# A hybrid convolution / mLSTM layer in float32: output projection by Strassen-Winograd pairs, branch stages reordered, small matmuls issued in groups

## The chip, the cores and the metric

The kernel runs on one core of a Trainium2 chip. Its time is the device time of one execution in microseconds (us); the time of before is the median of three runs, 2753.09 us (2752.79 to 2756.44). All durations below come from one profiled execution of the kernel before, which took 2749.06 us itself. Engines: PE is TensorE (matmuls), PEld its weight loads, DVE VectorE, ACT ScalarE, POOL GpSimd, SP the engine whose queue issues nearly all DMAs here.

## What is computed

One layer over 2048 tokens of 1024 channels. An input projection of some 11,000 columns feeds a gated short convolution (branch A) and a bidirectional chunked mLSTM with eight heads (branch B). Each branch has its own projection, gates merge them, and one output projection and a residual follow:

```python
y_a = b_a * conv * jax.nn.silu(z_a)
y_b = jax.nn.sigmoid(o) * hn * jax.nn.silu(z_b)
merged = jax.nn.sigmoid(g_a) * (y_a @ w_pa) + jax.nn.sigmoid(g_b) * (y_b @ w_pb)
out = merged @ w_out + b_out
x = x + gate[:, None, :] * out
return rmsnorm(x, g_final)
```

## The kernel before

Tokens are worked off in two halves of 1024. Every large product is done in float32 by splitting each operand into a rounded part and a rest (`split`, L178: an ACT cast, then a DVE or POOL subtract) and adding three matmuls, `PASSES`. One such matmul has a 128x128 weight and 512 moving columns; it is called a dense matmul below.

The input projection uses the seven products of Strassen-Winograd instead of eight (`pair`, L368; `Stream`, L293 makes the weight combinations on POOL, `total`, and splits them). A pair covers 256 output columns and one half of the tokens in 7x4x3 = 84 dense matmuls. Three PSUM banks X, Y, Z of the pool `pd` take the products in the order XYXYZYZ. The token combinations (`Tokens`, 14 pairs of buffers among `x0` to `x27`) are made once per half. For half 1 they go through DRAM (`prep_b`, `xod`).

The two branch projections (`branch`, `slab`, L419) and the output projection (`output`, L1292) do all eight block products. For each of eight column tiles (or token tiles) there are two accumulations of 8x3 = 24 dense matmuls, so 384 for each of the six stages at the end. Their moving operands are split once per stage into eight pairs of buffers (`Branch`, L1222), region 0 in `x0` to `x15`, region 1 in `x16` to `x27` and five to eight small buffers. The stages of before come in this order: branch A of half 1, branch B of half 1, output of half 1, branch A of half 0, branch B of half 0, output of half 0. `Branch(...)` issues all loads and splits of a stage in one block of code between two stages.

Beside the dense matmuls run the generators of two queues, `urgent` and `later`. `run(dense, rate, urate)` (L117) takes `rate` steps of `later` and `urate` steps of `urgent` per dense matmul; a step is the stretch of code up to the next `yield`. So the order on PE is fixed by these rates and yields. The order on the other engines is set by the scheduler, save for instructions that are held by `pin`. The longest generator is `scan` (L714), the emitting mLSTM pass: 64 chunks of 128 tokens (8 heads, 8 chunks) for each half. One chunk does a state update (L607, on a weighted copy `vw` that POOL makes at L602), scores (L764), four matmuls into `pn` (L813, L815), and, for four chunks at a time, four transposes (`finish`, L779). POOL masks the weights of two chunks (`mask`, L750) when their DMA `mw` has landed, and after that makes the next `vw`. These matmuls are in plain float32, have 128 or 129 columns and are called small below. In before, the scan of half 1 runs beside the input projection of half 1, and the scan of half 0 beside the first four of the six last stages.

## Time and profile before

| | |
|---|---|
| median of three runs | 2753.09 us |
| profiled execution, its own time | 2749.06 us |
| its span (first to last instruction) | 2747.3 us |
| PE busy | 2629.4 us, 96% |
| DVE, POOL, ACT busy | 61%, 42%, 39% |
| input projection of half 0, of half 1 | up to about 1070 us, up to about 2075 us |
| scan of half 0 | about 2075 to 2550 us |
| last stage | about 2655 to 2740 us |

A row of the windows view gives, for a stretch, its length, the busy time and (in brackets) the number of instructions on PE, PEld, DVE, ACT and POOL, the granted share of the TensorE clock, the DMA engines' share and their GB/s. A matmul's shown duration overlaps that of the next, so the price of one is read from the count in a full stretch or from the start times. A float32 small matmul shows as two records (x2), a transpose as one.

### The profile page before, as it was taken

To read this page: it belongs to the slowest core of one execution; us is meant where nothing else is said; L and a number is where in the kernel's file an instruction comes from. 1 tells how busy PE (TensorE), PEld (TensorE's weight loads), DVE (VectorE), ACT (ScalarE), POOL (GpSimd) and SP (SyncE) were. 2 spreads that over 40 slices of the span, in tenths; PEclk is the share of its full clock that TensorE was granted. 3 is DMA by queue.
4 is the path that set the end of the run, shared out by engine and by line. 5 is a ranking of instruction groups with operands and counts; after the bars stand their busy time and mean duration, and the time that the engine had idled before them with its cause. 6 is when DMAs were issued, how large, how long until landed. Compare 5 with 4: busy or idle time off the path is not lost. (4 is left out here: it accounts for less than half of the span.)

```text
span 2747.3 us, 38077 instructions
## 1 busy us (share of the span) xinstructions
PE 2629.4 (96%) x12715; PEld 2162.8 (79%) x12715; DVE 1673.9 (61%) x3022; ACT 1062.8 (39%) x2151; POOL 1160.4 (42%) x1387
## 2 busy tenths in 40 slices
PE   4799999999999999999999999999999998989998
PEld 3588888787788887787888888888888786778887
DVE  6743237688966657477677577568546554565423
ACT  6433334333344435343444444444445332332211
POOL 3521213363555542235555555545532354553123
PEclk8799999999999999999999999999999999999999
DMA  7223334363534557335545545644548777766753
GB/s 256 77 77 115 106 105 127 112 233 104 192 113 125 171 180 234 96 103 160 170 126 156 170 130 155 173 130 145 188 161 299 244 252 239 240 229 208 236 182 106
DMA packets 361659, 454.93 MB, mean 166 GB/s; under 512 B 24008, under 2 KB 261752, under 8 KB 361464
## 3 DMA queue, kind: packets, MB, share of 16 engines
q1 hardware_dynamic: 361072, 452.41, 51.9%
q8 instruction: 101, 1.65, 0.3%
q14 instruction: 94, 0.77, 0.1%
q10 hardware_dynamic: 392, 0.10, 0.0%
HBM read 324.08 MB, written 128.34 MB: 165 GB/s over the span
## 5 line engine op out<-in xcount | busy, mean ns | idle before, releaser
L384 PE MATMUL pd<-x,wh 128*128 128x512 f32 x4928 | 1628.4, 405 | 27.9 <-DVE u L393 12.5
L384 PEld LDWEIGHTS pd<-x,wh 128*128 128x128 f32 x4928 | 906.2, 189 | 215.2 <-DVE u L393 18.2
L384 PE MATMUL pd<-x,wl 128*128 128x512 f32 x2464 | 993.2, 403 | 0.8 <-DVE wl L180 0.8
L384 PEld LDWEIGHTS pd<-x,wl 128*128 128x128 f32 x2464 | 466.3, 189 | 87.9 <-DVE wl L180 1.2
L179 ACT CAST wh<-sw 128x512 fp32r<-128x512 f32 x352 | 218.1, 620 | 464.8 <-PE pd L384 402.9
L180 DVE TENSOR_TENSOR wl<-sw,wh 128x512 fp32r<-128x512 f32 x352 | 290.8, 827 | 173.0 <-ACT wh L179 172.5
L179 ACT CAST wh<-wr 128x512 fp32r<-128x512 f32 x328 | 203.2, 620 | 426.6 <-PE pd L384 290.8
L429 PE MATMUL pd<-x,wh 128*128 128x512 f32 x896 | 300.9, 420 | 2.1 <-DVE x L180 1.6
L328 POOL TENSOR_TENSOR sw<-wr,sw 128x512 f32<-128x512 f32 x88 | 120.5, 1369 | 430.8 <-DVE wl L180 427.1
L602 POOL TENSOR_SCALAR vw<-tk,wk 128x129 f32<-128x129 f32 x272 | 207.2, 770 | 189.9 <-DMA tk<-tokd 127.8
L180 DVE TENSOR_TENSOR wl<-wr,wh 128x512 fp32r<-128x512 f32 x328 | 258.7, 789 | 32.9 <-ACT wh L179 32.5
L328 POOL TENSOR_TENSOR sw<-wr 128x512 f32<-128x512 f32 x88 | 121.4, 1380 | 182.1 <-DVE wl L180 165.7
L429 PE MATMUL pd<-x,wl 128*128 128x512 f32 x448 | 172.3, 395 | 0.0
L429 PEld LDWEIGHTS pd<-x,wh 128*128 128x128 f32 x896 | 150.9, 191 | 21.2 <-DVE x L180 2.5
L846 DVE TENSOR_TENSOR t2k<-pd,u 128x512 f32<-128x512 f32 x168 | 115.5, 687 | 69.0 <-PE pd L384 67.3
L1312 PE MATMUL pd<-x,wh 128*128 128x512 f32 x448 | 152.1, 421 | 0.0
L250 POOL TENSOR_SCALAR ssq<-ssq 128x1 f32<-128x1 f32 x128 | 37.9, 296 | 240.9 <-ACT hf L829 236.0
L827 ACT ACTIVATE hf<-pn,rd 128x128 f32<-128x128 f32 x128 | 46.8, 366 | 239.4 <-DVE rd L823 161.9
L328 POOL TENSOR_TENSOR sw<-sw,wr 128x512 f32<-128x512 f32 x88 | 121.2, 1377 | 42.3 <-DVE wl L180 32.8
L328 POOL TENSOR_TENSOR sw<-wr,wr 128x512 f32<-128x512 f32 x88 | 127.4, 1448 | 15.4 <-DMA wr<-in_w_in_dram 10.0
L750 POOL TENSOR_SCALAR_AFFINE_SELECT mw<-mw 128x256 f32<-128x256 f32 x128 | 57.0, 465 | 177.4 <-DMA mw<-mwd 122.1
L813 PEld LDWEIGHTS pn<-tk,pt 128*128 128x128 f32 x512 | 95.8, 189 | 24.8 <-DVE pt L766 2.5
(276 smaller groups left out, 3716.8 us busy)
## 6 DMA issues: line engine op xcount, KB each, us to landing
wr<-in_w_in_dram SPq DMA_DIRECT2D x176, 512.0 KB, 3.9
mw<-mwd SPq DMA_DIRECT2D x64, 512.0 KB, 5.2
tk<-tokd SPq DMA_DIRECT2D x64, 386.0 KB, 4.1
tk<-tokd SPq DMA_DIRECT2D x64, 257.0 KB, 3.0
qkd<-t2k SPq DMA_DIRECT2D x64, 256.0 KB, 3.0
qk<-qkd SPq DMA_DIRECT2D x64, 256.0 KB, 3.4
tokd<-t2k SPq DMA_DIRECT2D x32, 258.0 KB, 3.3
tokd<-tk SPq DMA_DIRECT2D x64, 129.0 KB, 3.2
```

What stands on the lines that cost most here:

```text
L179: nc.scalar.copy(hi, raw)
L180: (eng or nc.vector).tensor_tensor(lo, raw, hi.bitcast(F32), op=OP.subtract)
L250: nc.gpsimd.tensor_scalar(dst, ss, 1.0 / n, EPS, op0=OP.mult, op1=OP.add)
L328: nc.gpsimd.tensor_tensor(s, a, b, op=op)
L384: nc.tensor.matmul(ps[b], op[wi][:, kk, :], xs.at(o, xi, kk), start=(fresh and kk + pi == 0), stop=(o == last[b] and kk == 3 and pi == 2), ...
L429: nc.tensor.matmul(pss[j], ops[k // 4][wi][:, k % 4, :], y(xi, k, j), start=(n + pi == 0), stop=(n == NK - 1 and pi == 2))
L602: pin(nc.gpsimd.tensor_scalar(vw, tk[:, VT], wk, None, op0=OP.mult))
L750: pin(nc.gpsimd.affine_select(mws[m][:, :, 0, d, :], mws[m][:, :, 0, d, :], pattern=[[0, 2], [s, P]], base=0, channel_multiplier=-s, compa ...
L813: nc.tensor.matmul(pn[:, d, :], pt[:, d, :], tk[:, VT], start=True, stop=False)
L827: nc.scalar.activation(hf, pn[:, 0, 0:P], AF.Copy, scale=rd[:, 0:1])
L846: nc.vector.tensor_tensor(t, ps, add, op=OP.add)
L1312: nc.tensor.matmul(pss[j], ops[k // 4][a][:, k % 4, :], wo(b, k, j), start=(k + pi == 0), stop=(k == NK - 1 and pi == 2))
```

## The change

- The output projection is done by `pair`: 8 pairs of token tiles, 7 products of 4x3 dense matmuls, 672 where 768 stood. Its fixed operand, `w_out` with the gate multiplied in, is stored by blocks (`wod`), three combinations are formed in DRAM by `combine` (the code that `prep_b` already had, now a function) beside the input projection of half 0, and it is loaded and split once, for both halves (`Operands`, the old `Tokens` with a loader).
- The order at the end is now A of half 1, B of half 1, A of half 0, B of half 0, then one output stage for both halves, half 1 first.
- `Branch` has a generator `fetch`: it issues the load of one block, waits 12 steps, then splits, with the casts held by `pin`. From the second branch stage on, operands come through `urgent` during the stage before. Gates and partial sums of a column tile are loaded when its accumulation begins (`PaEnd.begin`, `PbEnd.begin`), not when it ends.
- The scan of half 0 is split: heads 0 to 2 run beside the input projection of half 1, heads 3 to 7 beside the first three branch stages. The rates are 0.34 for 0.255 there, and 0.305 for 1/3 in the branch stages.
- Yields between single small matmuls are gone: four transposes come in a row, the four `pn` matmuls come in a row, and update and scores of the next chunk come in a row; `gap(4)` stands between such groups.

The core of the diff:

```diff
-    class Tokens:
+    class Operands:
...
+        def load(self, src, os):
+            for o in os:
+                for q in range(2):
+                    load_split(self.t[o][0][q], self.t[o][1][q], src[self.PLACE[o], :, 2 * q:2 * q + 2, :])
...
+    def combine(src, tile):
...
@@ scan
                 update(new, cur, tk, sp[n][2], g[carried]["dec"][:, j:j + 1])
-                yield
             if n + 1 < len(flat):
-                if n % 2:
-                    yield
                 start(n + 1)
-                yield
+            yield from gap(4)
             pt, qw, _ = sp.pop(n)
...
             for d in range(2):
                 nc.tensor.matmul(pn[:, d, :], pt[:, d, :], tk[:, VT], start=True, stop=False)
-                yield
                 nc.tensor.matmul(pn[:, d, :], qw[:, d, :], cur if d == carried else tk[:, ST], start=False, stop=True)
-                yield
+            yield from gap(4)
...
-        run(pair(st, xB, fin), 0.8 if w in ("q0", "o0", "z0") else 0.255, 0.5)
+        run(pair(st, xB, fin), 0.8 if w in ("q0", "o0", "z0") else 0.34, 0.5)
...
             later.extend([state_scan(sp_, hs, 1), scan(sp_, hs, 1)])
+            if r < EARLY:
+                later.append(scan(sp_, [r], 0))
...
-    def output(half, wo, misc):
...
+    later.append(scan(sp_, range(EARLY, NH), 0, lambda h: heads_done(h)))
+    RATE, URATE = 0.305, 0.3
...
+    ya = Branch(0, lambda k: yad[1][k])
+    yb = Branch(1, lambda k: ybd[1][k], ())
+    urgent.extend(yb.fetch(k) for k in range(NK))
+    run(branch(w_pa, ya, PaEnd, 1), RATE, URATE)
+    flush(urgent)
+    ya = Branch(0, lambda k: yad[0][k], ())
+    urgent.extend(ya.fetch(k) for k in range(NK))
+    run(branch(w_pb, yb, PbEnd, 1), RATE, URATE)
+    flush(urgent)
+    yb = Branch(1, lambda k: ybd[0][k], ())
+    urgent.extend(yb.fetch(k) for k in ready)
...
+    run(branch(w_pa, ya, PaEnd, 0), RATE, 0.5)
+    flush(later)
+    flush(urgent)
...
+    urgent.extend(load_wo(o) for o in range(4))
+    run(branch(w_pb, yb, PbEnd, 0), 0, 0.3)
+    flush(urgent)
+
+    def output():
+        tiles = [(half, 2 * p) for half in (1, 0) for p in range(4)]
+        st = Stream((mgd[half].rearrange("n p t -> (n p) t"), i * P, True) for half, i in tiles)
...
+        begin(0)
+        st.fill(3)
+        wo.claim(range(4, 7))
+        wo.load(wod, range(4, 7))
+        for m in range(len(tiles)):
+            for n, _ in enumerate(pair(st, wo, fin(m))):
+                if n == 30:
+                    begin(m + 1)
+                yield
```

How the scan stands on PE in the branch stages. Before, the end of one chunk's `pn` group, the next update (L607) and the next scores (L764), with L429 the dense matmuls of a branch:

```order
L815 MATMUL pn_21289<-cst_21184,qw_21198 128x129
L429 MATMUL pd_21298<-x_4732_19740,wh_21058 128x512
L429 MATMUL pd_21298<-x_4733_19741,wh_21058 128x512
L429 MATMUL pd_21298<-x_4732_19740,wl_21059 128x512
L607 MATMUL pu_21333<-vw_21284,tk_21175 128x129
L429 MATMUL pd_21298<-x_4734_19745,wh_21064 128x512
L429 MATMUL pd_21298<-x_4735_19746,wh_21064 128x512
L429 MATMUL pd_21298<-x_4734_19745,wl_21065 128x512
L764 MATMUL pa_21342<-qk_21177 128x128
```

Three dense matmuls stand between any two small ones; from the scores of a chunk, whose step also issues the next `vw`, to the update that reads it there are 15. Now (L855 and L856 are the `pn` matmuls, L472 the dense ones):

```order
L472 MATMUL pd_22108<-x_5064_20760,wh_21865 128x512
L855 MATMUL pn_22110<-tk_21802,pt_21998 128x129
L856 MATMUL pn_22110<-tk_21802,qw_22000 128x129
L855 MATMUL pn_22110<-tk_21802,pt_21998 128x129
L856 MATMUL pn_22110<-cst_21989,qw_22000 128x129
L472 MATMUL pd_22108<-x_5065_20761,wh_21865 128x512
```

The four stand in a row. And the update (L650) with the scores (L807) right behind it, 13 dense matmuls later:

```order
L472 MATMUL pd_22108<-x_5172_21207,wh_21871 128x512
L472 MATMUL pd_22108<-x_5173_21208,wh_21871 128x512
L650 MATMUL pu_22153<-vw_22087,tk_21978 128x129
L807 MATMUL pa_22159<-qk_21980 128x128
L472 MATMUL pd_22108<-x_5172_21207,wl_21872 128x512
```

From the scores to the next update there are now 26 dense matmuls. Counted over the whole program, small matmuls stand in 600 groups between dense ones, where there were 1427.

What ACT has before the copy of the first product's bank at the start of the output stage (L431; `x_5982` and the like are operand blocks of `w_out`, whose casts wait for their DMAs; `wh` are weight splits):

```order
L179 CAST wh_24819<-wr_24803 128x512
L179 CAST x_5982_24824<-x_5984_24826 128x1024
L179 CAST wh_24855<-sw_24853 128x512
L179 CAST x_5981_24823<-x_5983_24825 128x1024
L179 CAST wh_24876<-sw_24811 128x512
L179 CAST x_5985_24827<-x_5987_24829 128x1024
L431 COPY u_24872<-pd_24859 128x512
L179 CAST x_5986_24828<-x_5988_24830 128x1024
```

Before, ACT had the operand casts of the last output stage in the branch stage ahead of it (four of them and a weight split are shown), and there was no copy of a bank:

```order
L179 CAST x_5962_24784<-x_5963_24785 128x1024
L179 CAST x_5964_24789<-x_5965_24790 128x1024
L179 CAST x_5966_24794<-x_5967_24795 128x1024
L179 CAST wh_24915<-wr_24845 128x512
L179 CAST x_5968_24799<-x_5969_24800 128x1024
```

Three casts of the last three operand blocks now stand ahead of the copy, and those blocks' buffers come free only with the last accumulation of branch B of half 0.

## Rows read from the trace of the kernel before

**Rows 1.** The page: span, busy time by engine, and in 40 slices the busy tenths of PE.
```profile
span 2747.3 us, 38077 instructions
PE 2629.4 (96%) x12715; PEld 2162.8 (79%) x12715; DVE 1673.9 (61%) x3022; ACT 1062.8 (39%) x2151; POOL 1160.4 (42%) x1387
...
PE   4799999999999999999999999999999998989998
```
**Rows 2.** Windows by stage: the input projection of half 0 and of half 1, the four stages beside the scan of half 0, branch B of half 0, the last output stage (columns as told above).
```profile
340.00:1070.00 730.00, 719.21 (x3345) 588.88 (x3344) 496.05 (x718) 284.79 (x468) 323.01 (x291) 1.00 0.48 149
1070.00:2050.00 980.00, 971.55 (x4766) 800.56 (x4765) 658.27 (x1289) 416.99 (x874) 471.59 (x571) 1.00 0.49 151
2050.00:2560.00 510.00, 475.35 (x2425) 394.90 (x2424) 280.99 (x656) 180.57 (x474) 210.44 (x354) 0.98 0.73 241
2560.00:2650.00 90.00, 90.00 (x399) 74.53 (x398) 32.79 (x43) 17.85 (x26) 21.32 (x15) 1.00 0.65 215
2655.00:2740.00 85.00, 85.00 (x377) 70.30 (x375) 33.91 (x43) 18.62 (x44) 28.59 (x31) 1.00 0.43 144
```
**Rows 3.** Windows of 50 us, the three in which the granted clock was below 1 after the start.
```profile
2150.00:2200.00 50.00, 45.82 (x236) 38.46 (x236) 26.59 (x66) 18.71 (x47) 16.43 (x29) 0.97 0.74 246
...
2300.00:2350.00 50.00, 36.52 (x170) 29.54 (x169) 24.79 (x55) 17.65 (x46) 22.96 (x35) 0.86 0.80 263
...
2400.00:2450.00 50.00, 43.59 (x219) 36.02 (x218) 29.28 (x63) 17.46 (x53) 28.65 (x47) 0.93 0.59 199
```
**Rows 4.** The waits view of PE from 2050 to 2560 us, its longest entry: who waited for whom, total us, times, longest.
```profile
PE pu L607 <- POOL vw L602: 30.0, 11, 6.4
```
**Rows 5.** PE's timeline at the four longest of these waits: start us, us, instruction, idle before it and its releaser.
```profile
2193.23 0.60 PE L607 MATMUL pu<-vw,tk 128*128 128x129 f32 x2 [4.18 <-POOL vw L602]
...
2309.48 0.80 PE L607 MATMUL pu<-vw,tk 128*128 128x129 f32 x2 [6.45 <-POOL vw L602]
...
2331.90 0.80 PE L607 MATMUL pu<-vw,tk 128*128 128x129 f32 x2 [5.60 <-POOL vw L602]
...
2407.15 0.80 PE L607 MATMUL pu<-vw,tk 128*128 128x129 f32 x2 [4.13 <-POOL vw L602]
```
**Rows 6.** The timeline of the other engines before the first of them, at the change from branch A to branch B of half 1.
```profile
2188.57 1.22 DVE L180 TENSOR_TENSOR x<-x,x 128x1024 fp32r<-128x1024 f32 x1
...
2189.13 2.18 ACT L179 CAST x<-x 128x1024 fp32r<-128x1024 f32 x2
...
2190.57 2.01 POOL L831 TENSOR_SCALAR hb<-hb,ssq 128x128 f32<-128x128 f32 x1
2190.97 1.22 DVE L180 TENSOR_TENSOR x<-x,x 128x1024 fp32r<-128x1024 f32 x1
...
2192.56 1.21 POOL L602 TENSOR_SCALAR vw<-tk,wk 128x129 f32<-128x129 f32 x2
```
**Rows 7.** Line 831 alone: how many, duration in ns (least, median, most), first and last start.
```profile
L831 POOL TENSOR_SCALAR hb<-hb,ssq x128: 603/616/2006, 1289.0 to 2544.8; 128x128 f32<-128x128 f32 x128
```
**Rows 8.** The waits view of POOL, 2050 to 2560 us.
```profile
POOL mw L750 <- DMA mw<-mwd: 65.4, 23, 8.3
```
**Rows 9.** A window full of dense matmuls and little else.
```profile
2600.00:2700.00 100.00, 100.00 (x442) 82.80 (x442) 30.74 (x45) 16.97 (x36) 31.52 (x27) 1.00 0.55 177
```
**Rows 10.** PE's timeline with a small matmul of two records (L813) and a lone transpose (L618) among dense ones.
```profile
1702.16 0.38 PE L813 MATMUL pn<-tk,pt 128*128 128x129 f32 x2
1702.30 0.48 PE L384 MATMUL pd<-x,wl 128*128 128x512 f32 x1
1702.62 0.40 PE L384 MATMUL pd<-x,wh 128*128 128x512 f32 x1
1702.85 0.27 PE L618 MATMUL pa<-ident,t2k 128*128 128x128 f32 x1
1702.88 0.48 PE L384 MATMUL pd<-x,wh 128*128 128x512 f32 x1
1703.20 0.39 PE L384 MATMUL pd<-x,wl 128*128 128x512 f32 x1
```
**Rows 11.** Groups by line, from the page: busy us, mean ns, idle before. A weight split on DVE, a weight combination on POOL.
```profile
L180 DVE TENSOR_TENSOR wl<-wr,wh 128x512 fp32r<-128x512 f32 x328 | 258.7, 789 | 32.9 <-ACT wh L179 32.5
...
L328 POOL TENSOR_TENSOR sw<-wr,wr 128x512 f32<-128x512 f32 x88 | 127.4, 1448 | 15.4 <-DMA wr<-in_w_in_dram 10.0
```
**Rows 12.** The same view of the last output stage, 2655 us to the end.
```profile
L1303 POOL TENSOR_TENSOR x<-x,x 128x1024 f32<-128x1024 f32 x8 | 19.2, 2410 | 25.7 <-DMA x<-in_x_dram 24.2 <-DVE x L1331 1.5
...
L180 DVE TENSOR_TENSOR wl<-mg,wh 128x512 fp32r<-128x512 f32 (+1 forms) x14 | 14.5, 1045 | 19.9 <-ACT wh L179 19.9
L1331 DVE SCALAR_TENSOR_TENSOR x<-x,ss,x 128x512 f32<-128x512 f32 x16 | 11.3, 750 | 11.1 <-POOL ss L1328 11.1
L1319 DVE TENSOR_TENSOR x<-x,pd 128x512 f32<-128x512 f32 x16 | 10.9, 687 | 22.8 <-PE pd L1312 20.3 <-POOL x L1303 2.5
```
**Rows 13.** DMA issues by line: how often, KB each, median us from issue to landing.
```profile
ybd<-g SPq DMA_DIRECT2D x32, 256.0 KB, 3.6
...
x<-ybd SPq DMA_DIRECT2D x14, 512.0 KB, 6.0
x<-wod SPq DMA_DIRECT2D x14, 512.0 KB, 7.4
```

293 lines of the change are left out of this document (137 added, 156 removed).

## The prediction

> **What bounds the kernel now.** I read the page first: PE is busy 96% of the span, no other engine over 61% [rows 1]. So time goes only where PE does less work, the same work closer together, or waits less. The windows view by stage then says where PE is idle (length less PE's busy time): 730 - 719.2 = 10.8 us in half 0, 980 - 971.6 = 8.4 us in half 1, and 510 - 475.4 = 34.6 us in the four stages beside the scan of half 0, while branch B of half 0 and the last output stage, with no scan beside them, show none [rows 2]. The same stretch holds the only windows after the start with a granted clock below 1. PE had idled there (50 - 36.5 = 13.5 us in the worst), and the engine has two levels, 1.2 and 2.4 GHz, so a mean of 0.86 means that part of the window ran at 1.2. The work lost is 50 us x (0.03 + 0.14 + 0.07) = 12.0 us [rows 3]. Idle and clock together make 46.6 us lost in that stretch, or 0.73 us for each of its 64 chunks. The waits view says for what: 30.0 of the 34.6 us are the state update waiting for POOL's `vw`, 11 times [rows 4], and the four longest take 6.45, 5.60, 4.18 and 4.13 us [rows 5].
>
> Why is `vw` late? Two things stand before it in POOL's queue. The mask waits for its DMA `mw`, 65.4 us in 23 waits [rows 8], in an SP queue that also holds each stage's block of operand loads. And where a stage's operands are split in one block, DVE and ACT are full of 1024-column splits and casts (1.22 and about 1.1 us each), and a POOL scaling takes 2.01 us [rows 6] where its median is 0.616 [rows 7].
>
> **Fewer dense matmuls.** 768 - 672 = 96. In a full window 442 fit into 100 us, 0.226 us each [rows 9]: -21.7 us. PE has no idle time in the last stage to swallow that. (The Trainium skill, TensorE: Matmul & The Clock Gate, "Wait — 56ns, not 53.3ns?", gives 215.7 ns for 512 columns at the full clock; by that the term would be -20.7 us. The trace differs, and its row is used.)
>
> **Small matmuls in groups.** A lone transpose between dense matmuls: from the dense start at 1702.62 to the second dense start after it, 1703.20, are 0.58 us where two dense ones take 0.452, so it costs 0.128 us. A second record in a row costs 0.46 - 0.35 = 0.11 (1702.16 to 1702.62 against 1702.85 to 1703.20) [rows 10]. So every broken-up group wastes 0.018 us, and as the stamps are rounded to 0.01 us, 0.008 to 0.028. The order has 1427 - 600 = 827 groups fewer: 7 to 23 us, I take 0.015 each, -12 us.
>
> **The waits for `vw`.** From the step that issues a `vw` to its reader there were 15 dense matmuls and four `pn` matmuls, now 26 and four: 11 x 0.226 = 2.5 us more slack. The operand blocks come one at a time, about 40 dense matmuls (9 us) apart, and the output stage, with its extra loads, has no scan beside it. If only the slack counted, the four long waits would leave 6.45 + 5.60 + 4.18 + 4.13 - 4 x 2.5 = 10.4 us and the other seven (30.0 - 20.4 = 9.6 us, 1.4 each) nothing. Only 40 of 64 chunks stay in these stages: 6.5 us. Of the other waits there (34.6 - 30.0) 40/64 leaves 2.9, and with waits so short I leave a quarter of 12.0 x 40/64, hence 2 us, for the clock: about 12 us. The ends are 0 (nothing is late once blocks are spread) and 46.6 x 40/64 = 29 (the loss goes with the chunks). I take 12, as it is worked out from the single waits. So this term is -34.6 us, between -46.6 and -17.5.
>
> **Three heads moved.** 24 chunks go to the input projection of half 1, whose 64 chunks cost 8.4 us of idle, 0.13 each: +3.2 us. The matmuls themselves only change place. Ends: 0, and 24 x 0.73 = 17.5 if they cost there what they cost in the late stages.
>
> **The combinations of `w_out`.** 16 more POOL subtracts of about 1.45 us [rows 11], 23 us, stand beside the input projection of half 0, where POOL is busy 323 of 730 us. They wait for their loads in POOL's order and can hold up weight combinations behind them: 0 to 10.8 us (the idle of that stage once more), I take 1.5.
>
> **Two joints.** (a) Branch B of half 0 needs head 7 of the scan. Behind its last four transposes stand 6 dense matmuls of branch A and 42 of branch B, 10.9 us; the chain is a DVE product 0.7 (as a sum with a bank [rows 12]), a store 3.6, a load 6.0 [rows 13], a cast 0.55 (half of a 1024-column one [rows 6]) and a split 0.79 [rows 11]: 11.6 us. Before, branch B of half 0 also took head 7's block from a load behind its store, with no idle after it [rows 2]. 0 to 5 us, I take 1. (b) The output stage starts with the copy of the first bank behind three casts of `w_out` blocks on ACT, and the third product overwrites that bank 24 x 0.226 = 5.4 us after the start. The third cast's buffer comes free 12 dense matmuls (2.7 us) before the start, its load takes up to 7.4 us [rows 13], the cast 1.1 and the copy 0.6 [rows 6]: 6.4 us, 1.0 late, and the next bank's sum behind the next DVE split as much again. 0 to 10 us (if six loads stand behind each other), I take 2.
>
> **The output stage in steady state.** One pair takes PE 84 x 0.226 = 19.0 us. DVE has seven splits at 0.789 [rows 11] to 1.045, three adds of a held bank at the same price, six sums with a bank at 0.687 and four scalings at 0.750 [rows 12]: 15.0 to 17.6 us. POOL has four combinations at 1.45 [rows 11] and two residual adds at 2.41 [rows 12], 10.6 us and a few short ones. Both are hidden by PE, so I cost it at nothing. What it costs without that cover is a rival below. The tail after the last matmul has the same steps as before.
>
> **The sum.** -21.7 - 12 - 34.6 + 3.2 + 1.5 + 1 + 2 = -60.6 us. Against the profiled execution's own 2749.06 us that is 2688.5. The median of the runs shown is 4.0 us above that execution, so I predict 2692 us, 2.2% faster.
>
> **The rivals.**
> *A. The waits go with the chunks.* The late `mw` is a matter of SP's order: stores that wait stand ahead of loads, and that is not touched. For it speak the 23 waits [rows 8]; against it, that the same scan costs only 0.13 us a chunk beside the input projection, which has fewer stores. Then the term of the waits is -17.5 and that of the moved heads +17.5: -21.7 - 12 + 4.5 = -29, so 2724 us.
> *B. DVE and POOL exclude each other in the output stage.* The POOL scaling that lasted 2.01 us overlapped a DVE split of 1.22 us with two operands in SBUF, and 0.616 + 1.22 = 1.84 is near what it took [rows 6, 7]. If all such work of a pair went one after the other (splits, held adds and scalings 10.9 us on DVE, 10.6 us on POOL: 21.5 us), a pair would take 2.5 us more than PE's 19.0, 20 us in all: 2712. Against it: durations in rows 11 and 12 hold such waiting already, and beside the input projection the same seven splits and four combinations per pair cost PE next to nothing [rows 2]. The Trainium skill says it as a rule (SBUF — State Buffer, "Who interferes with whom"): a DVE instruction with two SBUF inputs and a GpSimd instruction that reads SBUF share one port pair, and whoever comes second is blocked for the whole instruction. By that rule the stage would be bound by the port, and the trace agrees on the one case above.
> *C. Slower.* One mechanism: the scan's waits spread to half 1. There 88 chunks, at rate 0.34 for 0.255, share SP, POOL and DVE with the weight stream. If each lost the 0.73 us of the late stages, half 1 would lose 64 us for 8.4, and the 40 late chunks 29 for 12: -60.6 - 3.2 + 55.6 + 17 = +9, so 2762. It decides from an average of (21.7 + 12 + 46.6 + 8.4 - 4.5) / 128 = 0.66 us over all 128 chunks. Now they lose (46.6 + 8.4) / 128 = 0.43; the wider slack speaks against it.
> *D. The waits vanish.* 0 for 12 and 0 for 3.2: 2677 us. For it: all four long waits lie at or near a change of stage or in the output stage beside the scan.
> That fewer matmuls would not come out is no rival: the order has 672.
>
> **How the numbers follow.** Chances: forecast 0.55 (its own range 2680 to 2706), A 0.15, B 0.10, C 0.05, D 0.15. The range goes from just below D to A: 2672 to 2727 us, which leaves C and the edges out. About 0.2%, 5.5 us, is what a measurement here can tell from no change. Only C, and A together with B and the worse ends of the joints, reach that: faster 0.92, same 0.03, slower 0.05.
>
> **What would show it.** Right: dense matmuls of the last stage 96 fewer with PE full there; waits of the update for `vw` under 8 us in the three branch stages beside the scan, and the granted clock near 1 there; idle of PE in half 1 under 14 us. Wrong: `vw` waits as long as before in the branch stages (A), a PE in the output stage that waits for splits or banks in every pair (B), or many short waits in half 1 (C).

## The result and the profile after

The changed kernel takes 2738.24 us (median of four runs, 2734.70 to 2744.29) against 2753.40 for the kernel before in the same session: ratio 0.9945, 95% interval 0.9926 to 0.9964. It is faster, by 15 us where 61 were predicted, and 2738 lies above the range of 2672 to 2727. One execution of `e18_best_steps`, of 7241 us where the others took 2692 to 2704, counts as slow and is left out of the numbers below. The profiled execution took 2744.29 us, 6 us above its median; that of before lay 4 us below its own. So the two traces differ by less (4.8 us in span) than the medians do.

The windows view of the changed kernel by stage (half 0, half 1, the three branch stages beside the scan, branch B of half 0, output of both halves) answers to [rows 2]:

```profile
340.00:1070.00 730.00, 710.49 (x3288) 585.63 (x3288) 494.61 (x695) 277.98 (x458) 343.20 (x301) 0.99 0.50 154
1070.00:2110.00 1040.00, 1014.70 (x5079) 847.14 (x5078) 703.18 (x1463) 447.89 (x989) 536.41 (x681) 0.99 0.52 160
2110.00:2460.00 350.00, 345.46 (x1767) 292.61 (x1767) 194.93 (x443) 124.22 (x309) 133.55 (x218) 0.99 0.79 258
2460.00:2555.00 95.00, 95.00 (x423) 78.69 (x422) 42.16 (x45) 19.52 (x27) 42.07 (x26) 1.00 0.82 268
2555.00:2735.00 180.00, 162.95 (x673) 129.74 (x671) 134.99 (x160) 62.72 (x129) 87.76 (x86) 0.95 0.37 126
```

The branch stages are nearly full now (4.5 us of idle). The output stage, full before, is not: 17 us of idle and a clock of 0.95. Both halves idle more than before: 19.5 for 10.8 us, and 25.3 for 8.4.

To compare stages with different work I count a **loss**: a stage's length less what its matmuls take where nothing holds them up. That is 0.2275 us for a dense matmul (390 of them take 88.6 us in branch B of half 0, where PE never waits), 0.11 for a small record and 0.12 for a 256-column one, and 0.012 for each change from dense to small. In most stretches of about 65 us without a wait this agrees to 0.5 us. A loss holds idle time and lost clock together.

| stage | before: us (loss) | after: us (loss) |
|---|---|---|
| input projection, half 0 | 996.2 (43.0) | 1010.7 (59.4) |
| input projection, half 1 | 997.6 (18.6) | 1050.5 (41.6) |
| stages beside the scan (before: with the output of half 1) | 487.8 (49.3) | 327.5 (9.7) |
| last stages without scan (before: branch B and output of half 0; after: branch B) | 180.3 (-0.3) | 88.6 (-0.3) |
| output, both halves | | 179.7 (26.8) |

Undisturbed work fell by 31.8 us and the branch stages' loss by 39.6. Given back were 16.4 in half 0, 23.0 in half 1 and 27 in the output stage. One trace has its scatter: among the runs below that leave a stage's code as it is, the loss lies between 56 and 62 us in half 0, 39 and 43 in half 1, 7 and 11 in the branch stages, 21 and 30 in the output stage.

The waits of PE say what each is (us in total, times, longest). Half 0, first the kernel before, then the changed one:

```profile
PE pd L384 <- DVE u L393: 10.1, 5, 4.2
```
```profile
PE pd L425 <- DVE u L434: 11.5, 6, 4.3
PE pd L425 <- DVE u L439: 6.9, 5, 3.3
```

Half 1, in the same order:

```profile
PE pn L607 <- POOL vw L602: 5.4, 6, 1.9
```
```profile
PE pn L650 <- POOL vw L645: 17.3, 13, 3.1
```

The branch stages beside the scan (answering to [rows 4]) and the output stage of the changed kernel; branch B of half 0 has none:

```profile
PE pu L650 <- POOL vw L645: 4.5, 1, 4.5
```
```profile
PE pd L425 <- DVE u L434: 11.2, 7, 2.2
PE pd L425 <- ACT u L431: 5.2, 1, 5.2
```

The wait for `vw`, 30.0 us in 11 before, is one wait in the branch stages. In half 1 the *state scan* (`state_scan`, the pass that only carries the states; its update stands at L650 under the tag `pn`) waits three times as long for its own `vw` as before. In the output stage and in half 0, PE waits for `u`, the copy or sum (L431, L434, L439) that frees a bank of a pair; in half 0 it did so before as well, and the waits on L439 are what came.

Timeline of the changed kernel in the output stage: its start, then a joint between two pairs:

```profile
2562.47 1.04 ACT L179 CAST x<-x 128x1024 fp32r<-128x1024 f32 x1 [0.33 <-DMA x<-wod]
2564.12 1.04 ACT L179 CAST x<-x 128x1024 fp32r<-128x1024 f32 x1
2565.07 0.58 ACT L431 COPY u<-pd 128x512 f32<-128x512 f32 x1
2565.70 1.22 PE L425 MATMUL pd<-x,wh 128*128 128x512 f32 x2 [5.23 <-ACT u L431]
...
2632.62 2.44 DVE L1389 SCALAR_TENSOR_TENSOR xt<-xt,ss,gf 128x512 f32<-128x512 f32 x2 [2.19 <-POOL ss L1387]
2636.19 0.68 DVE L434 TENSOR_TENSOR u<-pd,u 128x512 f32<-128x512 f32 x1
2636.92 0.73 PE L425 MATMUL pd<-x,wh 128*128 128x512 f32 x2 [1.72 <-DVE u L434]
```

At the start ACT's copy stands behind casts that wait for `w_out` blocks. At the joint DVE first waits 2.19 us for POOL's row scale, then scales the finished tile (2.44 us). After a split and an add, which the rows leave out, it makes the sum that PE needs. DVE waited for that row scale 25.8 us in 15 waits:

```profile
DVE xt L1389 <- POOL ss L1387: 25.8, 15, 2.2
```

The clock adds to it. In the 10 us that begin with the end of the 5.2 us wait the mean grant was 0.73, and PE did only 24 matmuls where a full 10 us holds 44 to 46; 2.0 us of the 10 were idle, the last 0.7 of that wait and a wait of 1.3:

```profile
2565.00:2575.00 10.00, 8.01 (x24) 6.12 (x25) 10.00 (x9) 5.27 (x8) 4.66 (x3) 0.73 0.26 94
2575.00:2585.00 10.00, 10.00 (x46) 8.28 (x45) 8.62 (x13) 3.90 (x10) 2.63 (x5) 1.00 0.23 76
```

### The profile page after: what moved, and what is told of

The parts are those of the page before. It is cut to its first block, busy times and chain, and to the rows that moved or that the text cites. A ratio compares the mean times of both kernels' runs of the same rounds, so it can differ in the third digit from the quotient of the medians.

```text
span 2742.5 us, 38093 instructions
## 1 busy us (share of the span) xinstructions
PE 2611.4 (95%) x12619; PEld 2167.1 (79%) x12619; DVE 1740.1 (63%) x3078; ACT 1075.7 (39%) x2175; POOL 1247.3 (45%) x1435
## 5 line engine op out<-in xcount | busy, mean ns | idle before, releaser
L425 PE MATMUL pd<-x,wh 128*128 128x512 f32 x5376 | 1730.7, 400 | 54.6 <-DVE u L434 28.2
L425 PEld LDWEIGHTS pd<-x,wh 128*128 128x128 f32 x5376 | 1001.9, 190 | 263.0 <-DVE u L434 36.1
L425 PE MATMUL pd<-x,wl 128*128 128x512 f32 x2688 | 1075.2, 400 | 0.8 <-DVE wl L182 0.8
L425 PEld LDWEIGHTS pd<-x,wl 128*128 128x128 f32 x2688 | 511.4, 190 | 103.2 <-DVE wl L182 1.2
L182 DVE TENSOR_TENSOR wl<-sw,wh 128x512 fp32r<-128x512 f32 x384 | 317.2, 827 | 194.2 <-ACT wh L179 187.9
L179 ACT CAST wh<-sw 128x512 fp32r<-128x512 f32 x384 | 237.7, 619 | 508.5 <-PE pd L425 436.8
L179 ACT CAST wh<-wr 128x512 fp32r<-128x512 f32 x352 | 217.8, 619 | 422.2 <-PE pd L425 277.0
L182 DVE TENSOR_TENSOR wl<-wr,wh 128x512 fp32r<-128x512 f32 x352 | 293.1, 833 | 43.8 <-ACT wh L179 43.4
L472 PE MATMUL pd<-x,wh 128*128 128x512 f32 x896 | 283.5, 398 | 0.0
L472 PEld LDWEIGHTS pd<-x,wh 128*128 128x128 f32 x896 | 167.6, 190 | 32.4
L472 PE MATMUL pd<-x,wl 128*128 128x512 f32 x448 | 174.6, 399 | 0.0
L369 POOL TENSOR_TENSOR sw<-wr,wr 128x512 f32<-128x512 f32 x96 | 138.1, 1438 | 18.8 <-DMA wr<-in_w_in_dram 12.4
L182 DVE TENSOR_TENSOR x<-x,x 128x1024 fp32r<-128x1024 f32 x72 | 90.8, 1272 | 49.7 <-ACT x L179 47.3
L894 DVE SCALAR_TENSOR_TENSOR t2k<-pd,cols,u 128x512 f32<-128x512 f32 x72 | 54.0, 750 | 84.6 <-PE pd L425 84.0
```

The lines of the kernel that those rows point to most:

```text
L179: i = nc.scalar.copy(hi, raw)
L182: (eng or nc.vector).tensor_tensor(lo, raw, hi.bitcast(F32), op=OP.subtract)
L369: nc.gpsimd.tensor_tensor(s, a, b, op=op)
L425: nc.tensor.matmul(ps[b], op[wi][:, kk, :], xs.at(o, xi, kk), start=(fresh and kk + pi == 0), stop=(o == last[b] and kk == 3 and pi == 2), ...
L472: nc.tensor.matmul(pss[j], ops[k // 4][wi][:, k % 4, :], y(xi, k, j), start=(k + pi == 0), stop=(k == NK - 1 and pi == 2))
L894: nc.vector.scalar_tensor_tensor(dst, ps, bcol(col), add, op0=OP.add, op1=OP.add)
```

## The experiments

The experiments start from the changed kernel, except the one on the order alone; ratios are to the kernel before, on the same chip.

### The output stage

**Scaling late** (`e1_scale_late`). The scaling of a pair is held back until the next pair's sum `u2`:

```diff
+        def close():
+            while due:
+                xt, row, rs = due.popleft()
                 for s in S2:
-                    nc.vector.scalar_tensor_tensor(xt[:, s], xt[:, s], rs, gf_t[:, s], op0=OP.mult, op1=OP.mult)
+                    pin(nc.vector.scalar_tensor_tensor(xt[:, s], xt[:, s], rs, gf_t[:, s], op0=OP.mult, op1=OP.mult))
                     ld.dma_start(out[row:row + P, s], xt[:, s])
```

> Edit: the final scaling of a pair of output tiles (L1389) and its two stores are emitted only behind the copy u2 of the next pair, so that no DVE instruction that waits for POOL's rs stands ahead of u2. Order theory (u2 stands in DVE's row behind a scaling that waits for POOL): the PE waits for u on L434 in the output stage, 11.2 us in 7 waits in the changed kernel, go, and with them the recurring part of the stage's loss; the time falls by 9 to 17 us, to about 2722 to 2730. Contention theory (DVE is merely slowed beside POOL, whatever its order): the waits on L434 stay within a third of 11.2 us and the time moves by less than 3 us. Both: the wait for ACT at the stage's start (5.2 us) stays.

Measured: 2728.8 us, ratio 0.9904 (0.9888 to 0.9919). The output stage's loss is 14.4 us for 26.8; the waits on L434 are 1.6 for 11.2, and the wait for ACT stays:

```profile
PE pd L425 <- ACT u L431: 5.0, 1, 5.0
PE pd L425 <- ACT wh L179: 4.2, 5, 1.4
PE pd L425 <- DVE u L434: 1.6, 1, 1.6
```

DVE has no less to do: it is busy for 135.1 us in 160 us of the stage, where it was 135.0 in 180. Its wait for the row scale, 25.8 us in 15, is one of 0.7. Its order was the cause of these 12 us.

**Splits late** (`e2_casts_late`). The splits of the last three `w_out` blocks stand behind the copies of the first pair:

```diff
-        wo.load(wod, range(4, 7))
+        for o in range(4, 7):
+            for q in range(2):
+                ld.dma_start(wo.t[o][1][q].bitcast(F32), wod[wo.PLACE[o], :, 2 * q:2 * q + 2, :])
...
+                    if o < 3:
+                        pin(nc.scalar.copy(wo.t[o + 4][0][q], wo.t[o + 4][1][q].bitcast(F32)))
```

> Edit: the cast and the subtraction that split the last three operand blocks of w_out are put, on ACT and DVE, behind the copies u of the first output pair. Queue theory (ACT's copy u stands behind three casts that wait for loads issued only when the branch's last buffers are free): the single wait of PE for ACT at the stage's start, 5.2 us, goes to under 1 us, and the clock in the stage's first 20 us stays near 1; the time falls by 5 to 8 us, to about 2731 to 2734. Landing theory (the loads themselves are late, products 4 to 6 need them): the wait only moves to products 4 to 6 as a wait for the blocks, and the time moves by less than 2 us.

Measured: 2737.24 us, 0.9935 (0.9921 to 0.9949). The wait for ACT is gone and a wait of 2.0 us for a later bank's sum (L439) has come; the stage loses 22.8 us for 26.8. That the copy stood behind the casts is shown, but the gain is less than the queue theory said, and within what runs of this stage differ by.

**Both** (`e12_both`), the two edits together.

> Edit: the scaling put behind the next pair's u2 and the last three splits put behind the first pair's copies, together. If both order theories hold, the output stage's loss of about 27 us falls to under 6 us and the time to about 2714 to 2722, the sum of the two single edits to within 3 us. If the stage is held by DVE's and POOL's shared work instead, the two together gain no more than the better of them, and the time stays above 2728.

Measured: 2718.7 us, 0.9868 (0.9849 to 0.9887). The loss is 9.1 us, not under 6. But in this stage the gains add up (17.7 us for 12.4 and 4.0; the time fell by 19.5 for 9.4 and 1.0, as other stages lost a little less too), and with the long waits gone the clock is 1.00 through the stage. The best kernel below has the same stage, with these waits:

```profile
PE pd L425 <- ACT wh L179: 3.3, 4, 1.2
PE pd L425 <- DVE xt L1382: 2.4, 1, 2.4
PE pd L425 <- DVE u L439: 1.4, 2, 0.9
```

### The moved heads and the state scan

**Scan put back** (`e3_scan_back`):

```diff
-    EARLY = 3
+    EARLY = 0
-        run(pair(st, xB, fin), 0.8 if w in ("q0", "o0", "z0") else 0.34, 0.5)
+        run(pair(st, xB, fin), 0.8 if w in ("q0", "o0", "z0") else 0.255, 0.5)
-    RATE, URATE = 0.305, 0.3
+    RATE, URATE = 0.485, 0.3
```

> Edit: the three heads' scan goes back out of the second half's input projection into the branch stages (EARLY 0, the rates 0.255 and 0.485 in place of 0.34 and 0.305); all the rest of the change stays. Slack theory (the higher rate leaves fewer dense matmuls between POOL's product and the matmul that reads it, so the move only carries the waits from the branch stages to the second half): the loss of the second half falls from 42 us back to about 20, that of the branch stages rises from 10 us to about 40 to 50, and the time stays within 10 us of 2738 (likeliest 2740 to 2748). Theory that the prediction rested on (the move removes about 35 us of waits in the branch stages and costs about 3 us in the second half): the time rises by 30 us, to about 2768, with the second half's loss unchanged. Theory that the waits of the branch stages came from the branch operands' loads and groups and not from the number of chunks: the loss in the branch stages stays near 10 us and the time falls to about 2718.

Measured: 2735.3 us, 0.9930 (0.9915 to 0.9945), no measurable change. Half 1 loses 24.4 us for 41.6, the branch stages 20.5 for 9.7. So moving the heads, with the rates that go with it, removed only 11 us in the branch stages and cost 17 in half 1: on its own it gained nothing. (Of the 24.4 us, 4.6 are one wait at the half's end for a scaling of the scan, `hb`, which the changed kernel does not have.) Eight heads beside the branches lose 20.5 us, not the 40 to 50 of the slack theory, so something else had taken most of the old waits.

**Together with the late output** (`e9_12_and_back`), this edit and `e12_both`.

> Edit: the scaling and the splits put late in the output stage (as in the run of both), and the three heads' scan put back into the branch stages (as in the run that did that alone). If the effects add up, since they lie in different stages: the 20 us of the first and the 3 to 6 us of the second, to about 2711 to 2716, the fastest so far. If the scan put back lengthens what the output stage starts from (its operands or copies late), the gain of the second part is lost and the time is 2718 or more.

Measured: 2720.34 us, 0.9877 (0.9858 to 0.9896), as `e12_both` alone. Moving the heads back was worth nothing here either.

**A step and the rates** (`e5_slack`). In the state scan two or three steps lie between POOL's `vw` and its update; at the rate 0.34 two steps are 5.9 dense matmuls, at the old 0.255 they were 7.8.

```diff
+            yield
             update(new, tk[:, ch - c0, ST], tk[:, ch - c0], vws.pop(n), g["dec"][:, j:j + 1], "pn")
...
-        run(pair(st, xA, fin), 0.235, 0.5)
+        run(pair(st, xA, fin), 0.26, 0.5)
...
-        run(pair(st, xB, fin), 0.8 if w in ("q0", "o0", "z0") else 0.34, 0.5)
+        run(pair(st, xB, fin), 0.8 if w in ("q0", "o0", "z0") else 0.36, 0.5)
```

> Edit: one more step between POOL's product vw and the state update that reads it in the state scan, the rates raised to 0.36 (second half) and 0.26 (first) so that the same work fits. Slack theory (the second half waits because too few dense matmuls lie between vw and the update, L650): the wait of PE for vw in the second half, 17.3 us in 13, falls below 6 us, the second half's loss from 42 to about 30, the time by 8 to 12 us; the first half does not change by more than 4 us. Rival (POOL gets to vw late, because its inputs land late or it has other work first, and the higher rate uses the step up): the wait stays above 12 us and the time within 4 us.

Measured: 2714.85 us, 0.9861 (0.9839 to 0.9884). Half 1 loses 25.6 us, as the slack theory said; half 0 loses 46.3 for 59.4, which it did not say. So the two edits were parted:

**The step alone** (`e6_step_alone`), the first `+` line of that diff.

> Edit: only the one more step between POOL's product vw and the state update in the state scan; the rates stay at 0.235 and 0.34. It parts the earlier run's two edits. Slack theory: the second half's loss falls from 42 to 26 to 32 us, as in that run; with more steps at the old rate some work is left over at the end of each half, done there with no dense matmul beside it, which costs 0 to 10 us; time 2722 to 2735. Rival (the rates did it: the work no longer left over, or other groups meeting other moments): the second half's loss stays at 38 us or more, time 2736 to 2750.

Measured: 2775.6 us, 1.0074 (1.0062 to 1.0086): slower than before. The state scan of half 0 needs more steps than the rate gives, and the rest runs after the last dense matmul, chunk by chunk at the pace of its loads (half 0 loses 94.8 us; one sixteenth of its dense work, the last, holds 39 of them). The windows of this kernel around that end, and the waits of PE in it:

```profile
1075.00:1090.00 15.00, 8.28 (x38) 6.47 (x36) 11.77 (x20) 8.34 (x11) 5.20 (x5) 0.89 0.74 227
1090.00:1123.00 33.00, 8.62 (x25) 6.12 (x25) 14.48 (x27) 5.22 (x5) 11.43 (x16) 0.50 0.71 211
...
PE pn L650 <- POOL vw L645: 26.7, 9, 7.5
```

Half 1, too, has a rest at its end: of the 39.4 us that it loses, the last of its sixteen parts holds about 20, and the other fifteen lose about 20 together where they lose 41 in the changed kernel. That agrees with the slack theory. The cost of leftover work was expected at 0 to 10 us and is nearly 40 in half 0 and 20 in half 1.

**The rates alone** (`e7_rates_alone`), the other lines.

> Edit: only the rates, 0.26 and 0.36 in place of 0.235 and 0.34; no further step in the state scan. Slack theory: a higher rate leaves fewer dense matmuls between vw and the update, so the second half's loss rises from 42 to 43 to 50 us; the first half may fall from 59 to 46 as in the run with both edits, since its loss is waits of dense products for copies u, not for vw; time 2728 to 2745. Rival (the rates did it): the second half's loss falls to 26 to 32 us and the time to 2713 to 2722.

Measured: 2738.78 us, 0.9946 (0.9934 to 0.9959). Half 1 loses 48.4 us: two steps are 5.6 dense matmuls now. Half 0 loses 48.7. The wait of the state scan's update in half 1, here and with the further step (8.3 dense matmuls):

```profile
PE pn L650 <- POOL vw L645: 22.2, 12, 4.1
```
```profile
PE pn L650 <- POOL vw L645: 4.7, 6, 1.3
```

The loss of half 1 follows the dense matmuls in two steps (three with the further step): 48.4 us at 5.6, 41.6 at 5.9, 24.4 at 7.8 (there with the heads moved back), 25.6 at 8.3. For half 0 it was the rates, not the step.

### The combinations of w_out

**Left out** (`e4_no_combine`); the output stage then reads plain blocks in the place of combined ones, so those combinations are not computed:

```diff
-        yield from combine(wod, big)
-        run(pair(st, xA, fin), 0.235, 0.5)
+        run(pair(st, xA, fin), 0.22, 0.5)
+    wo.PLACE = [0, 3, 2, 1, 0, 2, 3]
```

> Edit: the 16 POOL subtractions, eight loads and eight stores that make the combined blocks of w_out in the first half are left out, with their steps, and the half's rate goes back from 0.235 to 0.22; the output stage reads four plain blocks in the combined blocks' place, so the combinations of w_out's blocks are left out of what is computed. Theory that the combining lengthens the first half (its POOL work beside DVE's two-operand work makes the copies u late, and its steps raise the rate for everything else): the first half's loss goes from 59 us to about 43 to 47, the waits for u on L439 from 7 us to under 2, the time falls by 12 to 16 us. Rival, that the first half's extra loss comes from the small matmuls issued in groups of four rather than one by one: the loss stays above 54 us and the time falls by less than 5 us.

Measured: 2728.46 us, 0.9913 (0.9894 to 0.9931). Half 0 loses 48.8 us, the same as in the run of the rates alone, which keeps the combining; but the waits on L439 stay, 6.5 us for 6.9, against the theory. The two runs gain in different places. Between 620 and 744 us (two of sixteen parts with equal dense work) the changed kernel loses 17.5 us, the kernel before 8.7, the run of the rates 8.2, and this one 16. So these runs give no price for the combining by itself. They show that half 0 can lose as little as 46 to 49 us with it (`e5_slack`, `e7_rates_alone`), 3 to 6 more than before, and that it loses 6 more than before without it.

Between 620 and 750 us PE waits for `u` where DVE instructions of 1.7 to 2.3 us (the convolution, and the sums over the rows of `w_ada`, which make the gate) stand ahead of a pair's sum. An example in the changed kernel:

```profile
628.32 2.29 DVE L1169 SCALAR_TENSOR_TENSOR acc<-xb,sc,acc 128x1024 f32<-128x1024 f32 x1
630.53 1.74 DVE L962 SCALAR_TENSOR_TENSOR cv<-cv,cols,cv 128x504 f32<-128x504 f32 x1
632.19 0.68 DVE L434 TENSOR_TENSOR u<-pd,u 128x512 f32<-128x512 f32 x1
632.92 1.22 PE L425 MATMUL pd<-x,wh 128*128 128x512 f32 x2 [4.31 <-DVE u L434]
```

Such waits were there before the change too (10.1 us in 5). With another rate they may meet other moments. That the moment decides is read from these rows and was not tried by itself.

### What emptied the branch stages

**Operands in one block** (`e8_one_block`):

```diff
-    yb = Branch(1, lambda k: ybd[1][k], ())
-    urgent.extend(yb.fetch(k) for k in range(NK))
+    yb = Branch(1, lambda k: ybd[1][k])
...
-    ya = Branch(0, lambda k: yad[0][k], ())
-    urgent.extend(ya.fetch(k) for k in range(NK))
+    ya = Branch(0, lambda k: yad[0][k])
```

> Edit: the operands of the second and third branch stages are loaded and split in one block as each stage starts, in place of spread steps with a gap between load and split. Theory that the spread loads took away the branch stages' waits (in the kernel before, the block of splits at a stage's start kept DVE and POOL from the scan): the branch stages' loss rises from 10 us by 15 to 30 us, and the time by as much. Rival, that the waits went with the order of the stages (no output stage among them) and with the steps of the scan: the loss rises by less than 8 us.

Measured: 2742.75 us, 0.9960 (0.9944 to 0.9976); the branch stages lose 12.0 us for 9.7. With five heads beside the branches the spread loads took away 2 us at most, no more than runs of this stage differ by.

**Old steps** (`e11_old_steps`): in the branch stages only, the scan gets its old yields back, one behind every small matmul (the new last argument):

```diff
-    later.append(scan(sp_, range(EARLY, NH), 0, lambda h: heads_done(h)))
-    RATE, URATE = 0.305, 0.3
+    later.append(scan(sp_, range(EARLY, NH), 0, lambda h: heads_done(h), True))
+    RATE, URATE = 0.274, 0.3
```

> Edit: the scan that runs beside the branch stages gets back the steps of the kernel before (every small matmul a step of its own, so no groups), at a rate of 0.274 in place of 0.305 so that a chunk still lies beside about 27 dense matmuls; order of the stages, three heads moved and all else stay. Theory that the grouped steps took most of the branch stages' waits away (they put a fixed 8 steps between POOL's vw and the update): the branch stages' loss goes from 10 us back up by 12 to 25 us, besides some 5 us for the groups broken up. Rival, that the order of the stages did it (no output stage, with its DVE and POOL work, beside the scan): the loss without the broken groups stays below 16 us, the time within 8 us of 2738.

Measured: 2735.4 us, 0.9939 (0.9923 to 0.9955); the loss is 5.7 us. With five heads the steps are not the cause either.

**The order alone** (`e13_order_alone`), on the kernel before, eight products and all:

```diff
-    RATE = 1 / 3.0
+    RATE = 0.43
...
+    ya = Branch(0, lambda k: yad[0][k])
+    run(branch(w_pb, yb, pb_fin, 1), RATE)
+    run(branch(w_pa, ya, pa_fin, 0), RATE)
+    flush(later)
+    yb = Branch(1, lambda k: ybd[0][k])
...
-    run(branch(w_pb, yb, pb_fin, 1), RATE)
-    early = (0, 1, 2, 3, 6, 7)
-    ya = Branch(1, lambda k: yad[0][k], early)
-    run(output(1, wo, 24), RATE)
...
+    run(output(1, wo, 24), 0)
+    run(output(0, wo, 24), 0)
```

> Edit on the kernel before, nothing of the change else: the last stages run in the order branch A and B of half 1, branch A of half 0, branch B of half 0, then both halves' output (eight products, no scan beside them), at a rate of 0.43 in place of a third, so that all eight heads' scan still fits beside the three branch stages. Order theory (the waits came where the output of half 1, with its work on DVE and POOL, ran beside the scan): the loss of the stretch with the scan falls from 49 us in the kernel before to 15 to 28 (the run with the scan put back has 20.5 with all eight heads there), the wait of PE for vw from 30 to under 16 us, and the time to 2715 to 2738. Rival (the waits go with chunks per dense matmul, whatever the stage): the higher rate leaves the loss at 45 to 60 us and the time at 2750 to 2765. Rival, that the new way of loading and splitting the operands was needed too (the old block loads here stay): the loss falls by less than half, to 30 to 42 us, time 2735 to 2748.

Measured: 2738.6 us, 0.9938 (0.9924 to 0.9951). This edit alone gives as much as the whole change. The stretch beside the scan loses 32.1 us for 49.3, in the range of the last rival, with the wait for `vw` halved against [rows 4]; the output stage of eight products is full. Waits of PE beside the scan, and the window of the output:

```profile
PE pu L607 <- POOL vw L602: 15.5, 10, 3.9
PE pa L764 <- DMA qk<-qkd: 3.9, 1, 3.9
```
```profile
2555.00:2728.00 173.00, 173.00 (x765) 143.19 (x763) 70.27 (x93) 39.41 (x92) 57.86 (x63) 1.00 0.43 142
```

From 32.1 to the 20.5 of `e3_scan_back`, also with all eight heads, 12 us were open. Three runs undo one difference each, on top of that edit.

**Block loads with eight heads** (`e15_back_block`), the diffs of `e3_scan_back` and `e8_one_block`.

> Edit: the three heads' scan back in the branch stages (all eight heads there, as in the run that did that alone) and the operands of the second and third branch stage loaded and split in one block, as before the change. Load theory (with all eight heads beside the branches the block of casts on ACT holds up hf, POOL waits for it in ssq, and vw stands behind that): the branch stages' loss rises from the 20.5 us of the run with the scan put back to 29 to 36, the level of the run with the order alone (32.1); time 2742 to 2755. Rival (the loads do not matter, as with five heads): loss below 25 us, time 2731 to 2741.

Measured: 2746.07 us, 0.9961 (0.9947 to 0.9975). The loss is 27.8 us, between the two theories: 7 us more. But the mechanism of the load theory does not show. PE waits for `vw` no longer than in `e3_scan_back`. What is new is one wait of 5.8 us for `qk`, the scan's own load for its scores, and some lost clock; `e13_order_alone`, which has block loads too, has such a wait of 3.9 us. And POOL's wait for `hf`, which ACT makes on the way to a chunk's norm (`ssq`) and by which the theory went, is as long in the next run, whose loads are spread. The waits of PE in `e3_scan_back` and in this run, then those of POOL in this run and in the next:

```profile
PE pu L650 <- POOL vw L645: 12.3, 5, 6.9
```
```profile
PE pu L650 <- POOL vw L645: 11.4, 4, 7.0
PE pa L807 <- DMA qk<-qkd: 5.8, 1, 5.8
```
```profile
POOL ssq L252 <- ACT hf L870: 101.8, 43, 14.2
```
```profile
POOL ssq L252 <- ACT hf L885: 101.0, 48, 5.6
```

The loads of `qk` and the blocks of operands go through the same queue, SP's; that the block made `qk` late is argued from that and not shown.

**Old steps with eight heads** (`e16_back_steps`), the diffs of `e3_scan_back` and `e11_old_steps`, with the rate 0.435.

> Edit: the three heads' scan back in the branch stages, and that scan in the steps of the kernel before (each small matmul its own step), at a rate of 0.435. Step theory (with eight heads the grouped steps do keep vw ahead of the update): the loss of the branch stages rises from 20.5 to 29 to 36 us, besides about 4 us for broken groups. Rival (the steps do not matter, as with five heads): loss below 25 us besides those.

Measured: 2751.63 us, 0.9984 (0.9973 to 0.9995). The loss is 34.3 us, 14 more, and the wait for `vw` is 21.5 us where `e3_scan_back` has 12.3:

```profile
PE pu L650 <- POOL vw L645: 21.5, 12, 6.6
```

**Loads at the ends with eight heads** (`e17_back_ends`):

```diff
         def begin(self, j):
-            s = self.s[j] = t2k()
+            pass
+
+        def end(self, j, ps):
+            s = t2k()
             ld.dma_start(s, sad[self.half][self.n, :, S2[j]])
...
-            pin(nc.vector.scalar_tensor_tensor(s, s, 1.0, ps, op0=OP.add, op1=OP.mult))
+            nc.vector.scalar_tensor_tensor(s, s, 1.0, ps, op0=OP.add, op1=OP.mult)
```

The same is done in `PbEnd`, all on top of the diff of `e3_scan_back`.

> Edit: the three heads' scan back in the branch stages, and the gate tiles s (and the partial sums m) loaded at a product's end, as in the kernel before, in place of at its start. Ends theory (DVE and POOL, in order, wait at each end for these loads and the scan's work stands behind them): the loss of the branch stages rises from 20.5 to 29 to 36 us. Rival: it stays below 25 us, the time at 2731 to 2741.

Measured: 2732.43 us, 0.9911 (0.9896 to 0.9926), loss 18.3 us for 20.5. Where these loads stand did not matter here.

What the slack is worth can now be read, as the dense matmuls between the step that makes `vw` and its update, by the yields and the rate. With eight heads beside the branches the loss is 20.5 us at 16.5 (8 steps, rate 0.485), 34.3 at 11.5 (5 steps, 0.435), and 32.1 at 11.6 in the run of the order alone; the kernel before had 15, and the output stage beside the scan besides, and lost 49.3. With five heads it is 9.7 at 26 (8 steps, 0.305) and 5.7 at 18 (5 steps, 0.274). So the slack counts with eight heads and not with five. Between 18 and 16.5 the loss goes from 5.7 to 20.5 us, but the number of heads changes there too: whether fewer chunks help by themselves or the slack has an edge there, no run shows. The parts of the change replace each other, and their gains do not add up.

### The best version

**Step, rates and late output** (`e10_step_and_late`), the diffs of `e5_slack`, `e1_scale_late` and `e2_casts_late`.

> Edit: the further step in the state scan with the rates 0.36 and 0.26, and in the output stage the scaling and the splits put late. If the effects add up, as they lie in different stages (about 23 us and 20 us below the changed kernel): 2692 to 2700, output stage's loss 9 to 10 us, the halves' 46 and 26 us. If they overlap (the work that waited in one place now waits in the other): 2704 or more.

Measured: 2699.02 us, 0.9793 (0.9780 to 0.9806), faster than both kernels. Halves, branch stages and output lose 46.7, 26.3, 10.8 and 8.6 us. Its output window, with PE nearly full at full clock:

```profile
2530.00:2690.00 160.00, 152.93 (x667) 124.22 (x665) 135.84 (x158) 62.35 (x128) 94.31 (x86) 1.00 0.38 139
```

**With the old steps in addition** (`e18_best_steps`), and the diff of `e11_old_steps`.

> Edit: the run of the further step in the state scan with both late parts of the output stage, and in addition the scan beside the branch stages in the steps of the kernel before at a rate of 0.274 (as in the run of the old steps). If the effects add up, the branch stages' loss goes from 10.8 to about 6 us and the time from 2699 to 2692 to 2697. If the loss there was chance of position, 2697 to 2702.

Measured: 2701.80 us (median of four, 2692.34 to 2704.29), 0.9798 (0.9778 to 0.9818), the same as without them; the branch stages lose 9.5 us. The 5.7 seen before did not come again.

## Why the prediction was wrong, point by point

Of the signs named, `vw` waits of 4.5 us and a clock of 0.99 in the branch stages came out as right; 25.3 us of idle in half 1 for under 14, and an output stage that is not full, as wrong.

- *Fewer dense matmuls, small matmuls in groups* (-21.7 and -12 = -33.7): right. Counted as undisturbed work it is -31.8 us: 96 x 0.2275 = 21.8 and 827 x 0.012 = 9.9. The 0.012 was put in by me; an estimate by a fit to 713 stretches without a wait, in seven of the traces, gives 0.011. No run tried the groups by themselves as work.
- *The waits for `vw`* (-34.6, ends -46.6 and -17.5): the size is right (-39.6); the reason holds in part. The wider slack is shown to matter with eight heads (11.5 against 16.5 dense matmuls: 14 us), not with the five of the changed kernel. The largest single part, 17 us, is the output stage gone from beside the scan, which I had named without a price of its own. Spread loads are worth 7 us with eight heads, by a wait for `qk` and not for `vw`, and 2 at most with five. Rival A (0.73 us for each chunk, whatever the order) is refuted: all 64 chunks lose 20.5 us in `e3_scan_back`, where A has 46.6.
- *Three heads moved* (+3.2, ends 0 and 17.5): a step that failed. Half 1 lost 23.0 us more, 17 of them with this move. I priced 24 chunks at the idle that half 1 already had per chunk, and did not see that the rate, raised to fit them in, shortens every distance that the code counts in steps, so that other work in the same queue, the state scan, loses its slack. `e5_slack`, `e6_step_alone` and `e7_rates_alone` show it: with the heads still there, a further step of slack takes the loss back to 25.6. Rival C had the place (many short waits in half 1) but the wrong pass and three times the price. The 17.5 of rival A for these heads is close to the 17 measured, by luck: it was the loss per chunk of the late stages, another wait in another pass.
- *The combinations of `w_out`* (+1.5, end 10.8): undersized by 15 us: half 0 lost 16.4 more. I looked at POOL's order only; the waits are for DVE's sums and copies `u`. With another rate and the combining kept, 11 of the 16 go. The other 6 stay when the combining is left out, so they are not shown to be its price. Why 0.26 does better than 0.235, and where the 6 come from, stays open beyond the rows shown.
- *Joint a* (+1): no wait there. *Joint b* (+2, end 10): the mechanism was right, the wait was 5.2 us, and behind it came some 10 us at a mean grant of 0.73 that I had not counted. Taking the wait away gave 4 to 5 us in this stage.
- *The output stage in steady state* (costed at nothing): the step that failed without any price, and with joint b the largest shortfall, 25 us. I compared busy sums per pair (15.0 to 17.6 us on DVE against 19.0 on PE) and called the work hidden. A busy sum doesn't see order. The scaling waits for a chain through ACT and POOL, and the sum that PE needs stands behind it in DVE's row: 12 us of the stage's 27, shown by putting it behind. Joint b has 4 to 5; the rest, 9 us, stays in the best kernel, whose waits of PE there (for a weight split's cast, a held add and a sum) come to 7.1. As made, seven products took 179.7 us where eight take 173 to 175 (`e13_order_alone`); with both edits they take 162.
- *Rival B* (DVE and POOL exclude each other) gave a like price for the stage (20 us) by another mechanism, and falls: the runs with the late scaling keep all that work, and the loss goes from 27 to 14 us, with the late splits to 9. Its sign, waits for banks in most pairs, came, but the order gives the same sign. The stretching itself is there. A POOL subtraction that starts with a DVE split takes 2.34 us, where rows 11 have 1.45 on average, and the DVE split beside it takes 1.76 us, where the one shortly before takes 0.69, all in the changed kernel:

```profile
2562.79 0.69 DVE L182 TENSOR_TENSOR wl<-sw,wh 128x512 fp32r<-128x512 f32 x1
...
2563.55 1.23 DVE L182 TENSOR_TENSOR x<-x,x 128x1024 fp32r<-128x1024 f32 x1
2563.56 2.34 POOL L369 TENSOR_TENSOR sw<-wr,sw 128x512 f32<-128x512 f32 x1 [5.88 <-DVE wl L182]
...
2564.69 1.76 DVE L182 TENSOR_TENSOR wl<-sw,wh 128x512 fp32r<-128x512 f32 x1
```

The Trainium skill (SBUF — State Buffer, "Who interferes with whom") has a DVE instruction with two SBUF inputs contend with a GpSimd instruction that reads SBUF, and this pair of rows agrees. This contention did not set the pace: in the best kernel's output window PE is busy for 153 us of 160, though DVE and POOL, with whatever time they held each other up counted as busy, show 135.84 + 94.31 = 230.

The sum closes. Between the two traces 60.6 us were predicted and 4.8 measured, 56 short. Half 1 has 23.0 - 3.2 = 19.8 of them, half 0 16.4 - 1.5 = 14.9, the output stage 27 - 2 = 25 and the work 1.9; the branch stages gave 5.0 more than said, and joint a cost 1 less. The medians differ from the forecast by 46 only, as the changed kernel's trace lay 6 us above its median, and that of before 4 below its own, which the forecast had added.

## What to carry to other kernels

Where background work is paced by steps per matmul, a higher rate shortens every distance counted in steps: before raising it, count the dense matmuls left between each producer and its reader, in all passes of that queue, and see to it that no work is left when the dense matmuls end. Work that is hidden by its busy sum can still stand ahead of the instruction that frees a bank: put whatever waits for another engine behind it in that engine's row, as `e1_scale_late` did. And when a change has several parts, undo each alone: here one part, the order of the stages, was worth as much as all of them.

## What the runs showed of the hardware

Small work without dense matmuls beside it is dear twice over. In the 33 us at the end of half 0 in `e6_step_alone`, PE was busy for 8.62 us and the granted clock was 0.50, which is 1.2 GHz throughout; POOL waited up to 5.6 us for a pair's load, PE up to 7.5 for POOL, and nothing lay beside it on PE (the loads, casts and splits of half 1's operands ran in the same stretch; how far they slowed the pair's loads is not shown):

```profile
1095.82 1.25 POOL L645 TENSOR_SCALAR vw<-tk,wk 128x129 f32<-128x129 f32 x2 [5.58 <-DMA tk<-tokd]
1096.55 1.38 PE L650 MATMUL pn<-vw,tk 128*128 128x129 f32 x4 [7.47 <-POOL vw L645]
...
1105.63 2.24 POOL L645 TENSOR_SCALAR vw<-tk,wk 128x129 f32<-128x129 f32 x2 [4.07 <-DMA tk<-tokd]
```

I had put the same leftover at 0 to 10 us; the last sixteenth of half 0 lost 39.
